# A decoder layer: the attention scores of heads 2 to 4 as three float32r products of rounded queries and keys and their remainders

## The chip, the cores and the metric

The kernel runs on one core of one Trainium2 chip. The metric is the device time of one launch in microseconds (us). The kernel before was run three times; its time is the median of these runs. One more execution was taken by the hardware profiler, and all views shown below come from it.

## The reference

One layer of a decoder over 512 tokens of 1024 features, in float32: a mixer and a feed-forward part. The mixer has two groups: four heads of an mLSTM (256 features each) and a causal depthwise convolution of 31 taps over 1024 channels. Their outputs are joined and mapped back. The part that the change touches is the mLSTM's scores:

```python
qk = silu(causal_dwconv(qk_raw, qk_conv_w, qk_conv_b))       # 4 taps
q, k = split(qk, 2)                                           # 4 heads x 256
...
scores = einsum("bhtd,bhsd->bhts", q_, k_) * exp(dmat - m_t)  # d: 256 features
num = w_inter * einsum("bhtd,bhde->bhte", q_, C) + einsum("bhts,bhse->bhte", scores, v_)
den = w_inter * einsum("bhtd,bhd->bht", q_, n) + sum(scores)
h = num / maximum(abs(den), exp(-m_t))
h = rms_norm(h, ml_norm_g) * sigmoid(o_pre)
```

The kernel computes all of this over the whole length at once (a causal matrix of 512 x 512 for each head), without the running state.

## The kernel before, in words

**Tiles and names.** A tile of the pool `slots` holds 128 partitions x 512 float32; there are 36. A head's queries are two such tiles (`q_0c`, `q_1c`: 128 features each, all 512 tokens), and its keys two (`k_2c`, `k_3c`). The code counts heads from 0, the text from 1: code head 1 is the second head. Names in profile and order carry no head's number; they repeat for each head.

**Three products for one.** Large matrix products are not done in float32. `w_split` rounds a tile to float32r (`..h`, a copy on ACT, L191) and subtracts that from the tile to get a remainder (`..l`, on POOL or DVE, L192); `mm3` then makes three float32r matmuls on PE for each pair of tiles: h x h, h x l, l x h (L210). The projections `qko` and `vo`, the glu, the output projection and the feed-forward part go this way, with the weights split as they arrive. The scores are the exception: they multiply `k` and `q` as plain float32 (L544).

**A head.** For each head PE makes the projections `qko_0` to `qko_3` (24 matmuls of 512 columns each for a stretch, 8 features' tiles x 3). `conv4` takes each from PSUM: a first step on ACT (L502, `Identity`), three steps on DVE (L504), and Silu on ACT (L505). The scores `s` are made in four blocks of keys, `s_0` to `s_3`, of 512, 384, 256 and 128 columns, each as two matmuls (one for each 128 features). DVE multiplies each with the decay matrix `E` (L545). Then come the outputs `o_0` to `o_3`, 128 tokens each, with `v` (L555). For each, ACT takes the denominator (`dm`, L558) and copies the output out of PSUM (`hn`, L559), and squares it (`junko`, L560). Later `hn` is scaled, transposed (`hT`, L586) and split into `hh` and `hl` (L592, L593).

**Banks.** The outputs `o`, the scores `s`, the transposes `hT` and the helper `Mb` take turns in two banks of PSUM (pool `at`): what is written into a bank waits for the last reader of what stood in it two turns before. So `o_2` waits for the copy `hn_0<-o_0`, and `o_3` for `hn_0<-o_1`. The projections use four other banks. The split weights take turns in 20 buffers, which are ten pieces (h and l each).

**Order.** The order of PE's instructions and of SP's (which issues most weight loads) is that of the program: the generator functions of the heads are stepped by hand, so that the outputs of one head, the gates `vo` and the projections of the next stand in turn. The orders of ACT, DVE and POOL are set when the kernel is built, by the framework's scheduler, which estimates when each operation can run. Each of these engines then works strictly in its order. DVE and POOL also do the depthwise convolution (`cv`, `cs`, `ydl`, `ysum`) in the background of the mixer, and DVE the products that make the modulation (`junk<-ada`, whose loads ACT issues).

Of the kernel before, what the change touches and what calls it, by code (L numbers as in the profile page):

```python
# [10 lines left out]
F32 = mybir.dt.float32  # L11
F32R = mybir.dt.float32r
BF16 = mybir.dt.bfloat16
AF = mybir.ActivationFunctionType
ALU = mybir.AluOpType
PSUM = bass.MemoryType.PSUM

P = 128
# [37 lines left out]
def decoder_layer(ctx, tc, w_glu0, x, c, adaT, vecs, w_glu, w_qko, w_v0, w_vo, w_out, w_up, w_down, out):  # L56
    nc = tc.nc
    V, S, G, PE = nc.vector, nc.scalar, nc.gpsimd, nc.tensor
# [31 lines left out]
    def slot(name, dt=F32):  # L90
        return slots.tile([P, T], dt, tag="t", name=name)
# [8 lines left out]
    def mmbank(name):  # L100
        return psum.tile([P, T], F32, tag="mm", bufs=4, name=name)

    def atbank(name):
        return psum.tile([P, T], F32, tag="at", bufs=2, name=name)
# [41 lines left out]
    def vcol(name, i):  # L146
        a = VEC[name][0] + i
        return vec[:, a : a + 1]
# [58 lines left out]
    def mm3(ps, a, b, start, stop, again=False):  # L207

        for i, (l, r) in enumerate(((a[0], b[0]), (a[0], b[1]), (a[1], b[0]))):
            PE.matmul(ps, l, r, start=start and i == 0, stop=stop and i == 2, skip_group_check=again)  # L210
# [97 lines left out]
    def u_tiles(name):  # L308
        hi = upool.tile([P, KT, T], F32R, tag="uh", name=f"{name}h")
        lo = upool.tile([P, KT, T], F32R, tag="ul", name=f"{name}l")  # L310
        return hi, lo, [(hi[:, j, :], lo[:, j, :]) for j in range(KT)]

    _, _, u = u_tiles("u")
# [30 lines left out]
    parts = {}  # L344
# [13 lines left out]
    for k in range(KT):  # L358
# [11 lines left out]
        hi, lo = u[k]  # L370
# [65 lines left out]
    def proj(ps, pieces, off):  # L436
        for k in range(KT):
            mm3(ps, blk(pieces, off + k), u[k], k == 0, k == KT - 1)
# [4 lines left out]
    for i in range(G0 // 2, KT):  # L443
        glu_weights(i)
        for half in range(2):
            ps = mmbank(f"glu{i}_{half}")
# [48 lines left out]
            S.activation(part_of(gate, tt), ps[:, DH:], AF.Tanh, scale=0.5)  # L495
            yield

    def conv4(ps, i, name):

        t = slot(f"{name}c")  # L500
        w = lambda tap: vcol("qk_conv_w", tap * 16 + i)
        S.activation(t, ps, AF.Identity, bias=vcol("qk_conv_b", i), scale=w(3))  # L502
        for d in range(1, 4):
            last_e[0] = V.scalar_tensor_tensor(out=t[:, d:], in0=ps[:, : T - d], scalar=w(3 - d), in1=t[:, d:], op0=ALU.mult, op1=ALU.add)  # L504
        S.activation(t, t, AF.Silu)  # L505
        return t

    hy = [None] * (2 * KT)

# [8 lines left out]
    def head_proj(h, i):  # L518

        pieces, qs, ks, so = heads[h]  # L520
        ps = mmbank(f"qko{h}_{i}")
        proj(ps, pieces, i * KT)
        e = 2 * h + i % 2
        if i < 2:
            qs.append(conv4(ps, e, f"q{h}_{i}"))
        elif i < 4:
            ks.append(conv4(ps, 8 + e, f"k{h}_{i}"))
        else:
            t = slot(f"so{h}_{i}")
            S.activation(t, ps, AF.Tanh, scale=0.5)  # L530
            so.append(t)
# [4 lines left out]
    def attention(h):  # L536

        _, qs, ks, so = heads[h]

        for cc in range(NT):  # L540
            n = NS[cc]
            sp = atbank(f"s{h}_{cc}")
            for d in range(2):
                PE.matmul(sp[:, :n], ks[d][:, cc * P : (cc + 1) * P], qs[d][:, cc * P :], start=d == 0, stop=d == 1)  # L544
            last_e[0] = V.scalar_tensor_tensor(out=E[h][cc], in0=sp[:, :n], scalar=DH**-0.5, in1=E[h][cc], op0=ALU.mult, op1=ALU.mult)  # L545
            if cc in ((0, 2, 3) if h == 0 else (1, 3)):
                yield
        ssq = small.tile([P, NT], F32, tag="ssq", name=f"ssq{h}")
        dm = small.tile([P, NT], F32, tag="dm", name=f"dm{h}")
        hn = [slot(f"hn{h}_{i}") for i in range(2)]  # L550
        for tt in range(NT):
            o = atbank(f"o{h}_{tt}")
            for cc in range(tt + 1):
                a = (tt - cc) * P
                PE.matmul(o[:, : DH + 2], E[h][cc][:, a : a + P], vs[h][cc], start=cc == 0, stop=cc == tt)  # L555
            junk = small.tile([P, DH], BF16, tag="junk2", bufs=1, name=f"junko{h}_{tt}")
            hv = hn[tt // 2][:, (tt % 2) * DH : (tt % 2 + 1) * DH]
            S.activation(dm[:, tt : tt + 1], o[:, DH : DH + 1], AF.Abs)  # L558
            S.activation(hv, o[:, :DH], AF.Copy)  # L559
            S.activation(junk, hv, AF.Square, accum_out=ssq[:, tt : tt + 1])  # L560
            if h and tt % 2:
                V.scalar_tensor_tensor(out=hn[tt // 2], in0=so[tt // 2], scalar=1.0, in1=hn[tt // 2], op0=ALU.add, op1=ALU.mult)
            if tt in (1, 2):
                yield
        rd = small.tile([P, NT], F32, tag="rd", name=f"rd{h}")
        fac = small.tile([P, NT], F32, tag="fac", name=f"fac{h}")
        V.tensor_tensor(out=dm, in0=dm, in1=em[:, :, h], op=ALU.max)
        V.reciprocal(rd, dm)
        V.scalar_tensor_tensor(out=ssq, in0=ssq, scalar=1.0 / DH, in1=rd, op0=ALU.mult, op1=ALU.mult)
        V.tensor_tensor(out=ssq, in0=ssq, in1=rd, op=ALU.mult)  # L570
        G.tensor_scalar(out=ssq, in0=ssq, scalar1=EPS, scalar2=None, op0=ALU.add)
        G.tensor_tensor(out=fac, in0=ssq, in1=mhalf, op=ALU.pow)
        if h == H - 1:
            V.tensor_tensor(out=fac, in0=fac, in1=rd, op=ALU.mult)
        for tt in range(NT):
            hv = hn[tt // 2][:, (tt % 2) * DH : (tt % 2 + 1) * DH]
            if h == H - 1:
                S.activation(hv, hv, AF.Copy, scale=fac[:, tt : tt + 1])
                continue
            V.tensor_scalar(out=hv, in0=hv, scalar1=fac[:, tt : tt + 1], scalar2=rd[:, tt : tt + 1], op0=ALU.mult, op1=ALU.mult)  # L580
        yield
        for e in range(2):
            tp = atbank(f"hT{h}_{e}")
            for tt in range(NT):
                src = hn[tt // 2][:, (tt % 2) * DH + e * P : (tt % 2) * DH + (e + 1) * P]
                PE.transpose(tp[:, tt * P : (tt + 1) * P], src, ident)  # L586
            t = tp if h else so[e]
            if not h:
                V.scalar_tensor_tensor(out=t, in0=t, scalar=1.0, in1=tp, op0=ALU.add, op1=ALU.mult)
            hi, lo = slot(f"hh{h}_{e}", F32R), slot(f"hl{h}_{e}", F32R)  # L590
            g = ghalf[:, 2 * h + e : 2 * h + e + 1]
            S.activation(hi, t, AF.Copy, scale=g)  # L592
            last_lo[0] = V.scalar_tensor_tensor(out=lo, in0=t, scalar=g, in1=hi.bitcast(F32), op0=ALU.mult, op1=ALU.subtract)  # L593
            hy[2 * h + e] = (hi, lo)
# [37 lines left out]
    def make_E(h):  # L632
# [6 lines left out]
        for cc in range(NT):  # L639
            b = ga[:, cc, h : h + 1]  # L640
            S.activation(E[h][cc][:, :P], md[:, cc * P : (cc + 1) * P], AF.Exp, bias=b, scale=-1.0)
            if cc < NT - 1:
                S.activation(E[h][cc][:, P:], mb[:, (cc + 1) * P :], AF.Exp, bias=b, scale=-1.0)
    head_load(0)
    head_proj(0, 0)
    head_proj(0, 1)

    fps = atbank("fcum")
# [4 lines left out]
    V.tensor_copy(Fc, fv)  # L653
    V.tensor_tensor(out=ga, in0=gz[:, :, :H], in1=Fc, op=ALU.subtract)
    head_proj(0, 2)

    head_proj(0, 3)
# [178 lines left out]
    for h in range(H - 1):  # L836
        head_load(h + 1)
        steps = attention(h)
        if h == 0:
            head_proj(1, 0)  # L840
# [50 lines left out]
    tc.cur_priority -= LATER  # L891
    wo = {}
    steps = attention(H - 1)
    next(steps)
    mix_first(0)
# [224 lines left out]
    for i in range(NF):  # L1120
        if i < NE:
            pa, pg = early[i]
        else:
# [12 lines left out]
            for half in range(2):  # L1136
                ps = mmbank(f"up{i}_{half}")
# [227 lines left out]
```

## Time and profile before

| | |
|---|---|
| median of 3 runs | 770.94 us (770.82 to 772.68) |
| profiled execution | 771.52 us, with a span of 769.8 us |
| PE busy | 758.5 us (99%) |
| DVE busy | 573.7 us (75%) |
| POOL busy | 522.7 us (68%) |
| ACT busy | 408.4 us (53%) |
| granted clock of PE, mean | 0.998 |
| share of the scores (L544) in the chain that ended last | 2.3% |

How to read it: busy time is summed over the whole span, so an engine with a low share can still be late at one place. A row of a timeline has the start, the length, the engine, the line of the code, the operation, what it writes and reads, and how many records it joins; in brackets stands for how long the engine was idle before it and what ended that. A float32 matmul has two records, a float32r matmul one. A row of the waits has the total, the count and the longest. A row of the table of busy time has the stretch, its length, the busy time (with counts) of PE, PE's weight loads, DVE, ACT and POOL, then the granted clock, the share of the DMA engines and GB/s.

### The profile page before, as it was taken

Reading aid. Unit: us, or ns where it says so; the run is one execution under the profiler, and the core shown is the slowest. Engines: PE = TensorE matmul, PEld = TensorE weight load, DVE = VectorE, ACT = ScalarE, POOL = GpSimd, SP = SyncE. Lnnn points to the kernel's source line nnn. Section 1 sums busy time; section 2 is a strip of 40 time slices with the busy share of each in tenths; the row PEclk is TensorE's granted clock in tenths of the full one; section 3 lists DMA queues with packets and bytes.
Section 4 is the critical chain, followed back from the end, with each engine's and each line's share of the span. In section 5 each row is a group of like instructions: output and inputs, shape, how many; then the busy total and the mean of one; then the engine's idle time right before and its main releaser. Section 6 shows DMA issues by size and latency. Waiting matters only on the chain.

```text
span 769.8 us, 10292 instructions
## 1 busy us (share of the span) xinstructions
PE 758.5 (99%) x3562; PEld 630.5 (82%) x3562; DVE 573.7 (75%) x831; ACT 408.4 (53%) x780; POOL 522.7 (68%) x432
## 2 busy tenths in 40 slices
PE   8999999999999999999999999999999999999996
PEld 6788898878788788788888998888888888888885
DVE  5669999979979696476949797675765677654548
ACT  7585438585665645573334554434445246566633
POOL 4789759795494871645611467886978786599943
PEclk9999999999999999999999999999999999999999
DMA  8973214311131250655953655856686584896273
GB/s 317 347 277 126 100 56 140 135 54 56 54 111 55 110 181 38 246 192 164 378 193 135 246 185 196 301 213 232 221 302 220 215 294 145 303 399 239 96 242 141
DMA packets 40137, 147.34 MB, mean 191 GB/s; under 512 B 3826, under 2 KB 5266, under 8 KB 30484
## 3 DMA queue, kind: packets, MB, share of 16 engines
q1 hardware_dynamic: 26372, 94.50, 34.1%
q10 hardware_dynamic: 13712, 52.18, 18.8%
q8 instruction: 28, 0.46, 0.2%
q14 instruction: 25, 0.20, 0.1%
HBM read 126.59 MB, written 20.07 MB: 191 GB/s over the span
## 4 chain that ended last, share of the span: by engine, by line
PE 91%; DMA 2%; DVE 2%; POOL 2%; issue 1%; ACT 1%; DVEq 0%; POOLq 0%; ACTq 0%
PE up L210 31%; PE qko L210 13%; PE dn L210 10%; PE vo L210 9%; PE glu L210 7%; PE mixa L210 6%; PE mixb L210 6%; PE s L544 2%; PE o L555 2%; PE glu L356 2%; PE v L210 1%; DMA p<-spill_t 1%; DMA wglu<-in_w_glu 1%; POOL wglu_0l L192 0%; PE cps L159 0%
## 5 line engine op out<-in xcount | busy, mean ns | idle before, releaser
L767 DVE SCALAR_TENSOR_TENSOR cv<-gt,cvw,cv 128x485 f32<-128x485 f32 (+23 forms) x200 | 137.1, 731 | 2.9 <-ACT cv L755 1.3
L763 POOL TENSOR_TENSOR cs<-cs,cs 128x510 f32<-128x510 f32 (+3 forms) x32 | 42.1, 1318 | 0.1
L210 PE MATMUL up<-u2l,wup_0h 128*128 128x512 f32 (+1 forms) x100 | 36.5, 365 | 0.1
L210 PE MATMUL up<-u2h,wup_0h 128*128 128x512 f32 (+1 forms) x100 | 36.5, 365 | 0.0
L210 PE MATMUL up<-u2h,wup_1024h 128*128 128x512 f32 (+1 forms) x100 | 36.4, 364 | 0.0
L210 PE MATMUL up<-u2h,wup_0l 128*128 128x512 f32 (+1 forms) x100 | 36.4, 364 | 0.0
L210 PE MATMUL up<-u2l,wup_512h 128*128 128x512 f32 (+1 forms) x100 | 36.4, 364 | 0.0
L210 PE MATMUL up<-u2h,wup_512h 128*128 128x512 f32 (+1 forms) x100 | 36.4, 364 | 0.0
L210 PE MATMUL up<-u2h,wup_1536h 128*128 128x512 f32 (+1 forms) x100 | 36.4, 364 | 0.0
L210 PE MATMUL up<-u2l,wup_1536h 128*128 128x512 f32 (+1 forms) x100 | 36.4, 364 | 0.0
L210 PE MATMUL up<-u2h,wup_1536l 128*128 128x512 f32 (+1 forms) x100 | 36.4, 364 | 0.0
L210 PE MATMUL up<-u2h,wup_512l 128*128 128x512 f32 (+1 forms) x100 | 36.4, 364 | 0.0
L210 PE MATMUL up<-u2h,wup_1024l 128*128 128x512 f32 (+1 forms) x100 | 36.4, 364 | 0.0
L210 PE MATMUL up<-u2l,wup_1024h 128*128 128x512 f32 (+1 forms) x100 | 36.3, 363 | 0.0
L176 DVE SCALAR_TENSOR_TENSOR junk<-ada,cb 128x1024 bf16<-128x1024 f32 x20 | 30.1, 1506 | 4.9 <-DMA ada<-in_adaT 4.8
L192 POOL TENSOR_TENSOR wup_0l<-wup,wup_0h 128x512 fp32r<-128x512 f32 x19 | 29.3, 1543 | 4.5 <-ACT wup_0h L191 4.5
L192 POOL TENSOR_TENSOR wup_1024l<-wup,wup_1024h 128x512 fp32r<-128x512 f32 x19 | 25.0, 1318 | 9.4 <-ACT wup_1024h L191 9.4
L192 POOL TENSOR_TENSOR wup_1536l<-wup,wup_1536h 128x512 fp32r<-128x512 f32 x19 | 27.6, 1455 | 4.7 <-ACT wup_1536h L191 4.4
L761 ACT ACTIVATE cs<-gt,cvw 128x511 f32<-128x511 f32 (+4 forms) x40 | 27.2, 712 | 6.3 <-POOL cs L763 3.8
L1099 DVE TENSOR_TENSOR b<-b 128x512 f32<-128x512 f32 x11 | 19.4, 1760 | 11.3 <-POOL b L1098 11.3
L1098 POOL TENSOR_TENSOR b<-b 128x512 f32<-128x512 f32 x11 | 14.2, 1291 | 17.3 <-DVE b L1097 17.3
L336 DVE SCALAR_TENSOR_TENSOR junk<-ada,cps 128x1024 bf16<-128x1024 f32 x16 | 19.5, 1219 | 8.3 <-ACT cb L411 4.6
(1097 smaller groups left out, 2738.5 us busy)
## 6 DMA issues: line engine op xcount, KB each, us to landing
wup<-in_w_up SPq DMA_DIRECT2D x22, 1024.0 KB, 6.0
b<-in_w_down ACTq DMA_DIRECT2D x11, 1024.0 KB, 5.1
spill_t<-b ACTq DMA_DIRECT2D x11, 1024.0 KB, 3.9
ada<-in_adaT ACTq DMA_DIRECT2D x20, 512.0 KB, 4.0
wqko<-in_w_qko SPq DMA_DIRECT2D x9, 1024.0 KB, 4.8
ada<-in_adaT SPq DMA_DIRECT2D x16, 512.0 KB, 7.2
wo<-in_w_out SPq DMA_DIRECT2D x8, 1024.0 KB, 4.8
wvo<-in_w_vo SPq DMA_DIRECT2D x6, 1024.0 KB, 4.8
```

The source lines that it names most:

```text
L176: t = V.scalar_tensor_tensor(out=junk, in0=r, scalar=1.0, in1=cb, op0=ALU.mult, op1=ALU.mult, accum_out=mod[:, i : i + 1])
L192: (eng or G).tensor_tensor(out=lo[:, :n], in0=src, in1=hi[:, :n].bitcast(F32), op=ALU.subtract)
L210: PE.matmul(ps, l, r, start=start and i == 0, stop=stop and i == 2, skip_group_check=again)
L336: V.scalar_tensor_tensor(out=junk, in0=first[k][:, i * D : (i + 1) * D], scalar=1.0, in1=cps, op0=ALU.mult, op1=ALU.mult, accum_out=part[: ...
L356: PE.matmul(ps, blk(wk, i)[a], u[k][b], start=k == 0 and p == 0, stop=k == KT - 1 and p == 1)
L544: PE.matmul(sp[:, :n], ks[d][:, cc * P : (cc + 1) * P], qs[d][:, cc * P :], start=d == 0, stop=d == 1)
L555: PE.matmul(o[:, : DH + 2], E[h][cc][:, a : a + P], vs[h][cc], start=cc == 0, stop=cc == tt)
L761: S.activation(t[:, d:], cvx[j][:, : T - d], AF.Copy, scale=w(CK - 1 - d))
L763: G.tensor_tensor(out=side[:, d:], in0=side[:, d:], in1=t[:, d:], op=ALU.add)
L767: tap = V.scalar_tensor_tensor(out=cp[:, d:], in0=cvx[j][:, : T - d], scalar=w(CK - 1 - d), in1=cp[:, d:], op0=ALU.mult, op1=ALU.add)
L1098: G.tensor_tensor(out=b12, in0=b22, in1=b12, op=ALU.subtract)
L1099: V.tensor_tensor(out=b22, in0=b22, in1=b11, op=ALU.subtract)
```

## The change

For all heads but the first, `conv4` also rounds each query and key tile on ACT (`..h`) and takes the remainder on POOL (`..l`), and the scores use `mm3`. That is four more ACT copies and four more POOL subtractions a head, and for each block of scores six float32r matmuls in the place of two float32 ones. The first head's scores stay, and what is done with scores and outputs stays.

```diff
-    def conv4(ps, i, name):
+    def conv4(ps, i, name, parts):
...
         S.activation(t, t, AF.Silu)
-        return t
+        if not parts:
+            return t
+        hi, lo = slot(f"{name}h", F32R), slot(f"{name}l", F32R)
+        S.activation(hi, t, AF.Copy)
+        G.tensor_tensor(out=lo, in0=t, in1=hi.bitcast(F32), op=ALU.subtract)
+        return hi, lo
...
-            qs.append(conv4(ps, e, f"q{h}_{i}"))
+            qs.append(conv4(ps, e, f"q{h}_{i}", h > 0))
...
-            ks.append(conv4(ps, 8 + e, f"k{h}_{i}"))
+            ks.append(conv4(ps, 8 + e, f"k{h}_{i}", h > 0))
...
-                PE.matmul(sp[:, :n], ks[d][:, cc * P : (cc + 1) * P], qs[d][:, cc * P :], start=d == 0, stop=d == 1)
+                if h:
+                    mm3(sp[:, :n], [z[:, cc * P : (cc + 1) * P] for z in ks[d]], [z[:, cc * P :] for z in qs[d]], d == 0, d == 1)
+                else:
+                    PE.matmul(sp[:, :n], ks[d][:, cc * P : (cc + 1) * P], qs[d][:, cc * P :], start=d == 0, stop=d == 1)
```

Lines after this are shifted: L544 is L552 after, L555 is L563, L558 to L560 are L566 to L568; the new copy is L509, the new subtraction L510. PE's order is otherwise the same. The scheduler gives ACT, DVE and POOL other orders. Three places of ACT's order follow, each before and after.

ACT before, at the outputs of the first head (`o_0`, `o_1`), while `conv4` works on the second head's keys `k_2` and `k_3`:

```order
L505 ACTIVATE k_2c<-k_2c 128x512
L191 ACTIVATE wqko_0_512h<-wqko_0_2143 128x512
L502 ACTIVATE k_3c<-qko_3_1860,vec 128x512
L558 ACTIVATE dm_1897<-o_0_1900 128x1
L559 ACTIVATE hn_0_1898<-o_0_1900 128x256
L558 ACTIVATE dm_1897<-o_1_1906 128x1
L559 ACTIVATE hn_0_1898<-o_1_1906 128x256
...
L505 ACTIVATE k_3c<-k_3c 128x512
L494 ACTIVATE v_1961<-vo_0_1965 128x256
```

And after:

```order
L505 ACTIVATE k_2c<-k_2c 128x512
L191 ACTIVATE wqko_0_512h<-wqko_0_2159 128x512
L509 ACTIVATE k_2h<-k_2c 128x512
L566 ACTIVATE dm_1913<-o_0_1916 128x1
L502 ACTIVATE k_3c<-qko_3_1872,vec 128x512
L566 ACTIVATE dm_1913<-o_1_1922 128x1
L505 ACTIVATE k_3c<-k_3c 128x512
L509 ACTIVATE k_3h<-k_3c 128x512
L494 ACTIVATE v_1977<-vo_0_1981 128x256
L567 ACTIVATE hn_0_1914<-o_0_1916 128x256
L567 ACTIVATE hn_0_1914<-o_1_1922 128x256
```

The two copies `hn_0` out of the banks stood before Silu of k_3c (L505), and now stand behind it, behind the new rounding k_3h, and behind the copy of `vo_0`.

ACT before, at the outputs of the second head, while the third head's `k_2` is in work:

```order
L502 ACTIVATE k_2c<-qko_2_2299,vec 128x512
L558 ACTIVATE dm_2353<-o_0_2356 128x1
L559 ACTIVATE hn_0_2354<-o_0_2356 128x256
L558 ACTIVATE dm_2353<-o_1_2362 128x1
L559 ACTIVATE hn_0_2354<-o_1_2362 128x256
...
L191 ACTIVATE wqko_0_0h<-wqko_0_2608 128x512
L505 ACTIVATE k_2c<-k_2c 128x512
```

And after:

```order
L509 ACTIVATE q_1h<-q_1c 128x512
L566 ACTIVATE dm_2397<-o_0_2400 128x1
L502 ACTIVATE k_2c<-qko_2_2339,vec 128x512
L566 ACTIVATE dm_2397<-o_1_2406 128x1
L191 ACTIVATE wqko_0_0h<-wqko_0_2656 128x512
L505 ACTIVATE k_2c<-k_2c 128x512
L191 ACTIVATE wqko_0_512h<-wqko_0_2656 128x512
L509 ACTIVATE k_2h<-k_2c 128x512
L567 ACTIVATE hn_0_2398<-o_0_2400 128x256
L567 ACTIVATE hn_0_2398<-o_1_2406 128x256
```

Here the copies `hn_0` moved behind Silu of k_2c, two pieces of the next head's weights and the rounding k_2h.

At the outputs of the third head ACT's order after the change is (before it, `hn_0<-o_0` stood right behind the first `dm`):

```order
L502 ACTIVATE k_2c<-qko_2_2824,vec 128x512
L566 ACTIVATE dm_2860<-o_0_2863 128x1
L174 DMA ada_3219<-in_adaT 128x1024
L566 ACTIVATE dm_2860<-o_1_2869 128x1
L191 ACTIVATE wo_0_0h<-wo_0_3173 128x512
L174 DMA ada_3223<-in_adaT 128x1024
L505 ACTIVATE k_2c<-k_2c 128x512
L509 ACTIVATE k_2h<-k_2c 128x512
L567 ACTIVATE hn_0_2861<-o_0_2863 128x256
```

The copy moved behind two issues of loads, a piece of the output weights (`wo`), Silu of k_2c and k_2h. At the outputs of the last head the copies keep their place, as no projections of a next head follow.

## The prediction

> **What bounds the kernel now.** I read the page first, for the share of each engine, and then the waits of PE alone.
>
> ```profile
> span 769.8 us, 10292 instructions
> PE 758.5 (99%) x3562; PEld 630.5 (82%) x3562; DVE 573.7 (75%) x831; ACT 408.4 (53%) x780; POOL 522.7 (68%) x432
> ...
> PE cps L159 <- ACT crow L158: 3.0, 1, 3.0
> PE glu L356 <- ACT uh L397: 1.1, 1, 1.1
> PE s L544 <- DVE hl L593: 0.5, 1, 0.5
> PE xT L252 <- ACT xr L304: 0.3, 1, 0.3
> ...
> 732.00:763.50 31.50, 31.50 (x140) 25.76 (x138) 20.34 (x30) 13.32 (x30) 14.62 (x12) 1.00 0.58 201
> ```
>
> PE is busy for 758.5 of 769.8 us, and the whole list of its waits is four rows with 4.9 us. After the opening one wait is left, 0.5 us. The last row above is the table of busy time for the end of the program: PE is busy for all 31.50 us of it. So this kernel is as long as PE's list of matmuls. Two things follow: a matmul that becomes shorter is won whole, and a wait of PE, anywhere, is lost whole, since no later stretch has idle PE time that could absorb it. The change does something of both kinds.
>
> **The matmuls of the scores.** The next rows are PE's timeline around the scores of head 2 (the first four: the two wide products, each with its two halves of the key; the other four: the narrow ones), and four pieces of the chain of work with start and length, for streams of equal matmuls.
>
> ```profile
> 204.76 1.02 PE L544 MATMUL s<-q_0c,k_2c 128*128 128x512 f32 x2
> 205.62 1.02 PE L544 MATMUL s<-q_1c,k_3c 128*128 128x512 f32 x2
> 206.48 0.81 PE L544 MATMUL s<-q_0c,k_2c 128*128 128x384 f32 x2
> 207.12 0.49 PE L544 MATMUL s<-q_1c,k_3c 128*128 128x384 f32 x1
> ...
> 219.56 0.59 PE L544 MATMUL s<-q_0c,k_2c 128*128 128x256 f32 x2
> 219.99 0.59 PE L544 MATMUL s<-q_1c,k_3c 128*128 128x256 f32 x2
> 220.42 0.38 PE L544 MATMUL s<-q_0c,k_2c 128*128 128x128 f32 x2
> 220.64 0.39 PE L544 MATMUL s<-q_1c,k_3c 128*128 128x128 f32 x2
> ...
> 105.92 11.52 PE v L210 x96
> 152.31 5.46 PE qko L210 x24
> 213.39 0.87 PE hT L586 x8
> ```
>
> Durations overlap in a pipeline, so I go from start to start. A float32 product of 512 columns takes 205.62 - 204.76 = 0.86 us, of 384 columns 0.64, of 256 columns 0.43, of 128 columns 0.22. Each stands twice in a head: 2 x (0.86 + 0.64 + 0.43 + 0.22) = 4.30 us.
>
> The change puts six float32r matmuls in the place of each pair. At 512 columns one takes 5.46 / 24 = 0.227 us (the projections qko). At 264 columns one takes 11.52 / 96 = 0.120 (v); I take that for 256 too. For 384 I take the middle, 0.173. At 128 columns no float32r matmul occurs here. The nearest row is hT, float32 transposes of 128 columns with a weight load each, 0.87 / 8 = 0.109; 264 columns hardly cost more than that, as if a weight load for each matmul set a floor. I take 0.107. The ends: 0.06 if the time goes on falling with the columns (half of 0.120), and 0.22 if a 128 column product costs what the float32 one does.
>
> After: 6 x (0.227 + 0.173 + 0.120 + 0.107) = 3.76 us a head. By width that is -0.36, -0.25, -0.14 and +0.20: the narrowest product gets dearer. The sum is -0.54 us a head, **-1.6 us** for heads 2 to 4; with the ends, -2.5 to +0.4.
>
> [...]
>
> **The copies and subtractions.** Twelve ACT copies (0.52 us each, from start to start, below) are 6.2 us on an engine that is idle for almost half the time, and twelve POOL subtractions (1.3 us each) 15.6 us on one with 32% idle. As sums they are covered. k_3l, the last remainder that head 2's scores need, can be made by about 190 us, and the scores start at 204.76; 14 us of cover. What is not covered is a place in ACT's queue.
>
> PE's outputs o take turns in two banks with everything else of the attention, so `o_2` needs the bank that `o_0` leaves, and that is left when ACT has copied it out (`hn_0<-o_0`). Before, that copy comes early. After the change ACT's order has the copy behind the Silu of a key tile and the new rounding `..h` of that tile, and Silu waits for a chain of three steps on DVE. This stands in the order of the built program, it is no guess; what it costs is read from three places of the trace.
>
> ```profile
> 182.28 0.62 ACT L191 ACTIVATE wqko_512h<-wqko 128x512 fp32r<-128x512 f32 x1
> 182.80 0.76 ACT L502 ACTIVATE k_3c<-qko,vec 128x512 f32<-128x512 f32 x1
> 183.46 0.15 ACT L558 ACTIVATE dm<-o 128x1 f32<-128x1 f32 x1
> 183.51 0.38 ACT L559 ACTIVATE hn<-o 128x256 f32<-128x256 f32 x1
> 187.12 0.63 ACT L505 ACTIVATE k_3c<-k_3c 128x512 f32<-128x512 f32 x1 [1.96 <-DVE k_3c L504]
> 187.66 0.37 ACT L494 ACTIVATE v<-vo 128x256 f32<-128x256 f32 x1
> 187.93 0.37 ACT L495 ACTIVATE so<-vo 128x256 f32<-128x256 f32 x1
> ...
> 183.75 0.74 DVE L504 SCALAR_TENSOR_TENSOR k_3c<-qko,vec,k_3c 128x511 f32<-128x511 f32 x1
> 186.35 0.74 DVE L504 SCALAR_TENSOR_TENSOR k_3c<-qko,vec,k_3c 128x509 f32<-128x509 f32 x1
> ...
> 185.08 1.47 PE L555 MATMUL o<-v,E 128*128 128x258 f32 x6
> ```
>
> *First head's outputs (A).* Before: hn at 183.51, done by 183.89; `o_2` starts at 185.08 and waits for nothing. After: k_2h goes in ahead of k_3c's first step, which moves from 182.80 to about 183.37 and ends 0.66 later, 184.03. DVE's chain then starts 0.28 later than at 183.75 and ends at 186.35 + 0.74 + 0.28 = 187.4 (DVE's own order around it is unchanged). Then ACT: Silu 0.54 (187.12 to 187.66), k_3h 0.52, v 0.27, hn 0.38: 189.1. `o_2` could start at 185.08. PE waits **4.0 us**. It can hardly be less than 3.5: Silu was held by DVE before too.
>
> ```profile
> 230.55 0.38 ACT L559 ACTIVATE hn<-o 128x256 f32<-128x256 f32 x1
> 235.95 0.63 ACT L505 ACTIVATE k_2c<-k_2c 128x512 f32<-128x512 f32 x1 [3.22 <-DVE k_2c L504]
> 236.49 0.61 ACT L191 ACTIVATE wqko_512h<-wqko 128x512 fp32r<-128x512 f32 x1
> ...
> 233.12 0.59 PE L555 MATMUL o<-v,E 128*128 128x258 f32 x2
> ```
>
> *Second head's outputs (B).* Before: hn done at 230.93, `o_2` at 233.12. After, the copy stands behind k_2c's Silu, wqko_512h and k_2h. The high end has Silu where it was: 235.95 + 0.54 + 0.52 + 0.52 + 0.38 = 237.9, a wait of 4.8 us. The low end: wqko_512h takes the buffers of the tenth weight piece before it, which the last matmuls of qko_3 still read, and these end as `o_2` could start; so at least 0.52 + 0.52 + 0.38 = 1.4 us. I take **1.5**: in DVE's new order two steps of the depthwise convolution (cv) and one multiplication (hn) no longer stand within or just ahead of k_2c's chain, some 3 us at 0.65 to 1.06 us each, which brings Silu to about 232.9, ahead of the buffers.
>
> ```profile
> 281.14 0.38 ACT L559 ACTIVATE hn<-o 128x256 f32<-128x256 f32 x1
> 289.13 0.63 ACT L505 ACTIVATE k_2c<-k_2c 128x512 f32<-128x512 f32 x1 [3.25 <-DVE k_2c L504]
> ...
> 284.88 1.87 DVE L176 SCALAR_TENSOR_TENSOR junk<-ada,cb 128x1024 bf16<-128x1024 f32 x1
> ...
> 286.62 0.60 PE L555 MATMUL o<-v,E 128*128 128x258 f32 x2
> ```
>
> *Third head's outputs (C).* Again k_2c's Silu and k_2h come ahead of hn. With Silu where it was: 289.13 + 0.54 + 0.52 + 0.38 - 286.62 = 3.95 us. But DVE's new order has k_2c's second step ahead of the long junk row and hn's multiplication behind the chain, 0.66 + 1.0 us less: **2.2 us** (1 to 4: the junk row waits for a DMA that ACT issues in this very queue).
>
> In the last head the copy keeps its early place, and that head's scores still wait 0.5 us for hl. The other waits that the new orders could make (`o_3`, Mb and the next scores on their banks, the scores on ..l) have some us to spare by the same reading.
>
> **The clock.** A wait of 4 us may cost more than itself. These rows are the end of the program and the opening, the same eight transposes twice:
>
> ```profile
> 764.00:766.00 2.00, 0.00 (x0) 0.00 (x0) 1.72 (x5) 0.31 (x2) 0.55 (x1) 1.00 0.70 262
> 766.00:767.00 1.00, 0.00 (x0) 0.00 (x0) 0.63 (x1) 0.00 (x0) 0.00 (x0) 0.57 0.18 68
> ...
> 8.89 1.71 PE xT L267 x8
> 11.87 0.90 PE xT L267 x8
> ```
>
> PE's last matmul starts in the stretch that ends at 763.5, and the granted clock (the third number from the end) falls to about half soon after 766, some 2.6 us later. Wait A is longer than that, B and C are not. How long the clock then stays low no row shows. In the opening PE is still at about half its speed at 8.89 us (1.71 against 0.90) and at full speed at 11.87: 3 us at half speed are seen, which cost 1.5 us. Ends: 0, if the clock does not fall, and 2.5, if a slow stretch lasts 5 us. I take **1.5**.
>
> [...]
>
> **The sum.** -1.6 + 4.0 + 1.5 + 2.2 + 1.5 = +7.6 us. The profiled execution took 771.52 us (a span of 769.8 and 1.7 around it), 0.6 above the median of the runs. Against it 779.1; against the median of 770.94, which I forecast, **778.5 us**.
>
> **The rivals.**
>
> 1. *Faster.* The scores win and PE never waits: it would need ACT to reach hn before 185.08, 233.12 and 286.62. 770.94 - 1.6 = 769.3, or 768.4 with the 0.06 us price. It decides at place A: Silu of k_3c would have to end by 183.9, but DVE's first step of that chain starts only at 183.75. 6 in 100.
> 2. *Only the first wait.* The time that PE loses at A lets DVE, which keeps working, run ahead, and B and C shrink to their lows or to nothing: 770.94 - 1.6 + 4.0 = 773.3, and 774.8 with the clock. For it speaks that DVE is 75% busy and has work lying ready; against it that the weight buffers of B do not depend on DVE. 13 in 100.
> 3. *Longer waits.* B and C keep Silu's old place: 778.5 + 3.3 + 1.8 = 783.6. The rows of DVE's order speak against it. 6 in 100.
> 4. *Dear narrow products.* If the 128 column matmul costs 0.22, the scores cost +0.4 instead of -1.6, and the time is 780.5. The hT row speaks against it. 6 in 100.
> 5. *A cheap wait.* The three waits together come to about the 1.6 us that the scores win: no difference. It would take A at a third of what I read. 5 in 100.
>
> **How the numbers follow.** The forecast has 64 in 100. The range reaches down to rival 2 without the clock, 773, and up past rival 4 and to B and C with half of their excess, 782. What a measurement of this kernel can tell from no change is 0.3%, 2.3 us. Slower by more: forecast and rivals 2, 3, 4: 0.89. Same: rival 5, 0.05. Faster by 0.3% needs rival 1 at its lower end; of its 0.06 I count 0.03 as faster and 0.03 as same.
>
> **What would show it.** In the waits of PE after: a row for `o` on ACT `hn` (line 567), three times, the longest near 4 us, about 7.7 in all. In PE's timeline: six matmuls of 512 columns in 1.36 us and of 128 columns in 0.64 us. In ACT's timeline around 187: Silu, k_3h, v, then hn. In the table of busy time a granted clock below 1 for some us after A. If no wait on hn is listed, the forecast is wrong at its root; if A is there and the clock stays full, it is 1.5 too high.

## The result, and the profile after

The changed kernel takes 790.73 us (median of four runs, 788.87 to 791.45) against 770.88 us for the kernel before on the same chip. The ratio is 1.024 (95% interval 1.022 to 1.026), slower by 19.9 us. The forecast of 778.5 us had the sign and the first mechanism; the size is far above its range. The profiled execution of the changed kernel took 788.87 us, with a span of 787.1, 17.3 us more than the span before.

First the page's busy times in the changed kernel, then its waits of PE (total, count, longest).

```profile
PE 765.0 (97%) x3586; PEld 636.7 (81%) x3586; DVE 572.8 (73%) x831; ACT 417.1 (53%) x792; POOL 535.0 (68%) x444
```

```profile
PE o L563 <- ACT hn L567: 5.9, 2, 3.2
...
PE o L563 <- DVE E L553: 2.6, 1, 2.6
PE s L210 <- DVE hl L601: 2.6, 3, 1.8
PE xT L992 <- DVE u2l L1000: 1.0, 1, 1.0
```

Left out are the opening's row `cps`, 2.9 as before, and two rows of 0.4 and 0.3. The row on `hn` is the one that was forecast, with two waits instead of three. The rows on `E`, `hl` and `u2l` were not. And PE is *busy* for 6.5 us more than before, though its products have become cheaper. That is mainly the clock. The next rows are from the table of busy time (stretch, length, then PE, weight loads, DVE, ACT, POOL, granted clock, DMA share, GB/s). The second stretch of each pair is one at half clock, and the first is the 3.41 us ahead of it:

```profile
184.36:187.77 3.41, 0.89 (x4) 0.80 (x5) 3.41 (x6) 2.74 (x8) 1.56 (x2) 1.00 0.00 0
187.77:191.19 3.42, 3.42 (x10) 2.66 (x9) 3.42 (x6) 1.47 (x7) 0.00 (x0) 0.50 0.03 7
...
228.74:232.15 3.41, 0.78 (x5) 0.32 (x3) 3.41 (x4) 0.00 (x0) 1.83 (x2) 1.00 0.00 0
232.15:235.56 3.41, 3.41 (x8) 2.76 (x9) 3.34 (x6) 0.00 (x0) 0.00 (x0) 0.50 0.00 0
...
283.35:286.76 3.41, 1.33 (x8) 0.76 (x6) 2.46 (x5) 3.38 (x7) 2.51 (x2) 1.00 0.01 2
286.76:293.59 6.83, 6.79 (x19) 5.64 (x20) 6.10 (x10) 0.52 (x2) 2.56 (x2) 0.50 0.26 77
```

Three times a stretch in which PE was busy for 0.8 to 1.3 of 3.41 us is followed by a stretch at half clock, of 3.4, 3.4 and 6.8 us. In these 13.7 us PE does about the work of 6.8: in the last of them a matmul of 512 columns starts 0.43 us after the one before it, against 0.23 at full clock.

Where PE fell behind is read from starts. In the next rows, PE in the changed kernel, each pair is the last matmul before a gap and the first after it.

```profile
183.82 0.39 PE L210 MATMUL vo<-wvo_1536h,ul 128*128 128x512 f32 x1
186.88 0.92 PE L563 MATMUL o<-v,E 128*128 128x258 f32 x3 [2.68 <-ACT hn L567]
...
229.13 0.39 PE L210 MATMUL qko<-uh,wqko_512l 128*128 128x512 f32 x1
232.15 0.80 PE L563 MATMUL o<-v,E 128*128 128x258 f32 x1 [2.63 <-DVE E L553]
...
240.45 0.39 PE L210 MATMUL qko<-uh,wqko_1536l 128*128 128x512 f32 x1
244.07 0.70 PE L563 MATMUL o<-v,E 128*128 128x258 f32 x2 [3.23 <-ACT hn L567]
...
283.33 0.39 PE L210 MATMUL qko<-uh,wqko_1536l 128*128 128x512 f32 x1
285.51 0.39 PE L210 MATMUL s<-q_0h,k_2h 128*128 128x256 f32 x1 [1.79 <-DVE hl L601]
```

A matmul of 512 columns starts 0.23 us after the one before it; what is beyond that is lost: 2.8 + 2.8 + 3.4 + 2.0 = 11.0 us. With 6.8 for the clock and 1.0 for `u2l` that is 18.8. Less about 1.3 for the cheaper products and 1.1 for the glu's wait in the opening, which is in the list of before and not in this one, 16.4 of the 17.3 us are found; the rest is small waits and rounding. The row on `u2l` isn't of the change alone: it comes with 0.6 and 0.7 us in two profiles below that lose nothing else.

The scores themselves do what they should. PE's timeline in the changed kernel, the first product of the 512 column and of the 128 column block, and the matmul that follows each block's six:

```profile
208.29 0.39 PE L210 MATMUL s<-q_0h,k_2h 128*128 128x512 f32 x1
...
209.65 0.33 PE L210 MATMUL s<-q_0h,k_2h 128*128 128x384 f32 x1
...
223.24 0.22 PE L210 MATMUL s<-q_0h,k_2h 128*128 128x128 f32 x1
...
223.86 0.45 PE L210 MATMUL qko<-uh,wqko_0h 128*128 128x512 f32 x1
```

Six of 512 columns take 209.65 - 208.29 = 1.36 us and six of 128 columns 0.62, where the prediction named 1.36 and 0.64.

**The two unforeseen waits** have one origin, the transposes `hT` of the outputs, while the next head's first query tile is in work. ACT splits `hT` into `hh`, DVE makes the remainder `hl`, and PE's next matmuls need these, or what stands behind them on DVE. ACT, DVE and POOL in the changed kernel, first head's transposes:

```profile
220.43 1.28 ACT L505 ACT_TABLE_LOAD   x1 [2.96 <-DVE q_0c L504]
221.72 0.64 ACT L505 ACTIVATE q_0c<-q_0c 128x512 f32<-128x512 f32 x1
222.39 0.63 ACT L509 ACTIVATE q_0h<-q_0c 128x512 fp32r<-128x512 f32 x1
222.93 0.71 ACT L600 ACTIVATE hh<-so,ghalf 128x512 fp32r<-128x512 f32 x1
...
223.67 7.45 DVE L601 SCALAR_TENSOR_TENSOR hl<-so,ghalf,hh 128x512 fp32r<-128x512 f32 x1 [1.13 <-ACT hh L600]
...
223.07 1.29 POOL L192 TENSOR_TENSOR wvo_1536l<-wvo,wvo_1536h 128x512 fp32r<-128x512 f32 x1
229.32 1.25 POOL L192 TENSOR_TENSOR wvo_1024l<-wvo,wvo_1024h 128x512 fp32r<-128x512 f32 x1
```

ACT has `hh` behind a table load (1.28 us), Silu and the new rounding; before, it stood right behind `q_0c`'s first step (217.01 in the trace before, with the two `hl` of 1.65 and 1.11 us right after). Then `hl` takes 7.45 us instead of 1.1 to 1.7: it ends 0.55 us after a row of POOL operations that run back to back from before its start. `E`, which the second head's `o_0` multiplies, stands behind it on DVE, and PE waits until 232.15. In the third head the late `hh` holds the scores directly (285.51).

### The profile page after: what moved, and what is told of

Same layout as the page of the kernel before. It is cut to its first block, busy times and chain, and to the rows that moved or that the text cites. A ratio compares the mean times of both kernels' runs of the same rounds, so it can differ in the third digit from the quotient of the medians.

```text
span 787.1 us, 10381 instructions
## 1 busy us (share of the span) xinstructions
PE 765.0 (97%) x3586; PEld 636.7 (81%) x3586; DVE 572.8 (73%) x831; ACT 417.1 (53%) x792; POOL 535.0 (68%) x444
## 4 chain that ended last, share of the span: by engine, by line
PE 69%; DVE 12%; DMA 7%; ACT 5%; issue 3%; POOL 3%; ACTq 0%; SPq 0%; DVEq 0%; POOLq 0%
PE up L210 31%; PE dn L210 9%; PE vo L210 8%; PE glu L210 7%; PE mixa L210 4%; DVE cv L775 4%; PE qko L210 2%; DMA wup<-in_w_up 2%; PE o L563 2%; PE glu L356 2%; DMA x<-in_x 2%; PE s L210 1%; DVE hl L601 1%; PE v L210 1%; DMA p<-spill_t 1%
## 5 line engine op out<-in xcount | busy, mean ns | idle before, releaser
L775 DVE SCALAR_TENSOR_TENSOR cv<-gt,cvw,cv 128x502 f32<-128x502 f32 (+22 forms) x200 | 136.9, 729 | 2.6 <-ACT cv L763 1.3
L563 PE MATMUL o<-v,E 128*128 128x258 f32 x80 | 21.7, 413 | 8.6 <-ACT hn L567 5.9
L563 PEld LDWEIGHTS o<-v,E 128*128 128x128 f32 x80 | 15.8, 201 | 12.8 <-ACT hn L567 7.2
```

Source lines behind the costliest of these rows:

```text
L775: tap = V.scalar_tensor_tensor(out=cp[:, d:], in0=cvx[j][:, : T - d], scalar=w(CK - 1 - d), in1=cp[:, d:], op0=ALU.mult, op1=ALU.add)
```

## The experiments

Three theories stood against each other. *Order*: the scheduler hands out the pool's tiles in the order in which the program first writes them, so new `..h` tiles that are written early push the copies `hn` and `hh` back, whether or not they bring work. *Work*: twelve more ACT copies and twelve more POOL subtractions are the cost. *Products*: the matmuls themselves are dearer.

### The products alone

The queries and keys of heads 2 to 4 are rounded in place, and their remainders are not made (each product uses the rounded tile for both), so that PE has all its new matmuls and no other engine has anything new.

```diff
-        t = slot(f"{name}c")
+        t = slot(f"{name}c", F32R if parts else F32)
...
-        hi, lo = slot(f"{name}h", F32R), slot(f"{name}l", F32R)
-        S.activation(hi, t, AF.Copy)
-        G.tensor_tensor(out=lo, in0=t, in1=hi.bitcast(F32), op=ALU.subtract)
-        return hi, lo
+        return (t, t) if parts else t
```

> The products of the change alone: heads 2 to 4 multiply rounded queries and keys three times (the remainders are left out, and the steps of the four-tap convolution write rounded values in place), so PE has the changed kernel's 36 matmuls a head at the new widths, and ACT and POOL have not one instruction more than before. If the loss comes from the orders and not from the products, the time is 769.5 us: 1.3 to 1.6 us less than before (in the changed kernel the four wide blocks took 0.55 us less and the four narrow ones 0.1 more for each head). If the products themselves cost more than their rows say, it stays above 771.

769.79 us against 771.2; the ratio is 0.998 (0.9965 to 0.9995). The waits of PE are those of the kernel before (`cps` 2.9, glu 1.0, `u2l` 0.6, `hl` 0.4). So the products bring -1.4 us (-2.7 to -0.4), and the theory that they are dearer falls.

### A new tile without new work

The remainders are left out again, and Silu writes its result, rounded, into a new tile instead of in place. No engine has an instruction more than in the kernel with the products alone.

```diff
+        if parts:
+            r = slot(f"{name}h", F32R)
+            S.activation(r, t, AF.Silu)
+            return r, r
         S.activation(t, t, AF.Silu)
-        if not parts:
-            return t
-        hi, lo = ...
+        return t
```

> As the run with the products alone, but Silu writes its rounded result into a tile of its own instead of in place (remainders left out again). No instruction is added on ACT or POOL; only one more tile is taken from the pool for each query and key. Theory order: the scheduler hands out tiles in the order in which the program first writes them, so the copies that free PE's banks stand behind Silu of the key again, and PE waits as in the changed kernel: 775 to 788 us. Rival work: the loss is the time that twelve copies and twelve subtractions take on ACT and POOL; without them nothing is lost: 769.5 us.

781.15 us (779.5 to 790.5); the ratio is 1.015 (1.009 to 1.021). Here are the waits of PE, and then the timelines of ACT at the first head's outputs (Silu is now the row that writes `k_3h`) and of DVE at its transposes:

```profile
PE o L562 <- ACT hn L566: 5.6, 3, 2.5
PE o L562 <- DVE E L552: 2.6, 1, 2.6
PE s L210 <- DVE hl L600: 1.9, 3, 1.1
```

```profile
181.16 0.22 ACT L565 ACTIVATE dm<-o 128x1 f32<-128x1 f32 x2
184.88 0.63 ACT L507 ACTIVATE k_3h<-k_3c 128x512 fp32r<-128x512 f32 x1 [3.51 <-DVE k_3c L504]
185.42 0.64 ACT L566 ACTIVATE hn<-o 128x256 f32<-128x256 f32 x2
...
220.49 7.31 DVE L600 SCALAR_TENSOR_TENSOR hl<-so,ghalf,hh 128x512 fp32r<-128x512 f32 x1 [1.24 <-ACT hh L599]
```

The same three waits are back, and the long `hl` too, with nothing added to ACT or POOL. ACT stands idle for 3.51 us ahead of Silu, with `o_0` and `o_1` ready to be copied (it has taken `dm` from both). So ACT had time for `hn`, not the turn. The work theory falls, and the order theory holds: a new tile, written early, is enough. How the scheduler comes to the new order was not looked into; that it is the handing out of tiles fits this run and the next, and is not shown beyond that. In the profiled execution the granted clock stays full to the end of the work (mean 0.998). Between the medians of this and the changed kernel lie 9.6 us, and the clock's 6.8 would be the larger part of them; the slowest of this kernel's four runs, 790.5 us, is also the one with the lowest mean clock, 0.990 against 0.994 to 0.998.

### All the work, written later

Everything of the change is kept. `conv4` only queues the two steps that split a tile; `flush` issues them after the outputs of the head before (keys) or after its transposes (first query tile).

```diff
-        S.activation(hi, t, AF.Copy)
-        G.tensor_tensor(out=lo, in0=t, in1=hi.bitcast(F32), op=ALU.subtract)
-        return hi, lo
+        def split():
+            hi, lo = slot(f"{name}h", F32R), slot(f"{name}l", F32R)
+            S.activation(hi, t, AF.Copy)
+            G.tensor_tensor(out=lo, in0=t, in1=hi.bitcast(F32), op=ALU.subtract)
+            pair.extend((hi, lo))
+        waiting.append(split)
+        return pair
...
         next(steps)
+        flush()
```

> The changed kernel with all its work (twelve copies, twelve subtractions, three products), but the program writes the rounding and the remainder of a key tile after the attention's outputs, and those of the first query tile after the transposes; ACT's order then has hn and hh about where they stood before. Theory order: the waits on hn and hl go, and the time is 769.5 to 772 us (at the third head one wait of a us or two could stay). Rival work: the same instructions cost the same time wherever they stand: 785 to 791 us.

770.18 us against 771.2; the ratio is 0.9986 (0.9977 to 0.9995). Of PE's waits one row is new, 0.5 us of `o` on `hn`; the others are those of the kernel before. Here is ACT's timeline at the first head's outputs:

```profile
184.17 0.38 ACT L582 ACTIVATE hn<-o 128x256 f32<-128x256 f32 x1
184.44 0.63 ACT L513 ACTIVATE k_2h<-k_2c 128x512 fp32r<-128x512 f32 x1
```

`hn` is back ahead of the rounding, the whole loss is gone, and the products' gain remains. This version beats both kernels, by a little. A second measurement of it, with more executions:

> The version with the splits written late once more, in more rounds beside it. Theory: as in the first time, 0.05 to 0.25% under before. Rival: the first result was chance, and the interval holds 1.

770.32 us against 771.83; the ratio is 0.9978 (0.9962 to 0.9994). The added copies and subtractions are covered, as the prediction said of their sums.

### One half at a time

If the order theory holds in detail, the keys' tiles push `hn` and the first query tile's push `hh`. In two kernels only the one or the other is written later.

```diff
+HOLD = "k"      # the other kernel: "q"
...
+        waiting.append(split)
+        if name[0] not in HOLD:
+            flush()
```

> The changed kernel with all its work, but only the key tiles' rounding is written after the attention's outputs; the query tiles' stays where the change has it, so hn comes early again and hh stays late. Theory order, piece by piece: the waits of o on hn (2.8 and 3.4 us) go; the long hl (7.4 us), PE's wait for E and the wait of the third head's scores on hl stay, each with a low clock behind it: 776 to 783 us. Rival: one of the two places carries all, 770 or 790 us.

> The other half: only the first query tile's rounding is written after the transposes (hh early), the key tiles' stays where the change has it (hn late). Theory order: hl takes 1 to 2 us, PE's wait for E and the scores' wait on hl go; the waits of o on hn stay, 2.8 us at the first head with a low clock behind it and 1.5 to 3.5 us at the second, and one at the third of up to 3: 776 to 783 us. Rival: as in the other half, 770 or 790 us.

With the keys later: 778.51 us, ratio 1.009 (1.006 to 1.012). With the queries later: 784.65 us, ratio 1.018 (1.014 to 1.021). One row of PE's waits from each, the keys' first:

```profile
PE s L211 <- DVE hl L616: 3.5, 2, 3.0
```

```profile
PE o L578 <- ACT hn L582: 9.9, 3, 4.7
```

Where the keys are written later no wait on `hn` is left, and the third head's scores wait 3.0 us for `hl`. Where the queries are, all three waits on `hn` are there (gaps of 4.9, 1.7 and 3.8 us at the places A, B and C), and `hl` is harmless. So the two kinds of waits belong to the two kinds of tiles. One thing came otherwise than expected: with the keys later the first head's long `hl` and PE's wait for `E` are gone too, though `hh` stands behind Silu and `q_0h` as in the changed kernel. DVE's row there:

```profile
221.22 1.16 DVE L616 SCALAR_TENSOR_TENSOR hl<-so,ghalf,hh 128x512 fp32r<-128x512 f32 x1 [0.88 <-ACT hh L615]
```

So a late `hh` alone doesn't make `hl` long. The losses, 6.9 and 13.1 us, add up to about that of the change, 19.9, but by chance, as their parts are not those of the changed kernel: the wait for `E` is in neither, A and C are longer than in its profile above (2.8 and 0.2 us), and B is shorter (3.4). The queries' kernel also lies a little above the 776 to 783 us that were expected. A differs from one execution to the next (below); why C and B differ no run isolates.

### The long remainder

Is the 7.45 us `hl` a matter of its operands? In the other heads the operand `hT` is in PSUM. Here the first head's gated output stays in PSUM as well; all else is as in the changed kernel.

```diff
-            t = tp if h else so[e]
+            t = tp
...
-                V.scalar_tensor_tensor(out=t, in0=t, scalar=1.0, in1=tp, op0=ALU.add, op1=ALU.mult)
+                V.scalar_tensor_tensor(out=t, in0=so[e], scalar=1.0, in1=tp, op0=ALU.add, op1=ALU.mult)
```

> The changed kernel, but the first head's gated outputs stay in the PSUM bank of their transposes instead of going back to an SBUF tile, so hl reads one operand from PSUM and one from SBUF, as it does for the other heads. Theory port: hl took 7.45 us because both operands were in SBUF while POOL ran six subtractions without a pause; now it takes 0.75, PE's wait for E (2.7 us) and the low clock behind it (1.7 us) go, and the time is 784 to 787 us. Rival: hl was long for another reason (its place, its rounding to float32r): it stays above 5 us and the time near 790.

788.06 us, ratio 1.023 (1.020 to 1.025). DVE's row at that place, then one row of the waits of PE and one of PE's timeline:

```profile
224.83 0.75 DVE L601 SCALAR_TENSOR_TENSOR hl<-hT,ghalf,hh 128x512 fp32r<-128x512 f32 x1 [1.09 <-ACT hh L600]
```

```profile
PE o L563 <- ACT hn L567: 5.6, 2, 4.8
...
225.72 0.36 PE L210 MATMUL s<-q_0h,k_2h 128*128 128x256 f32 x1 [1.83 <-DVE hl L601]
```

On the operand the answer is plain: 0.75 us, and the wait on `E` is gone. On the time the edit gave less than the expected 784 to 787 us. A has 4.8 us here, and the edit brings a wait of its own: `hl` now reads the bank of the transposes, and the second head's scores, which need that bank, wait 1.8 us for it (the last row). So this run doesn't price the long `hl` alone. What the two engines would share no run shows; the word port in the expectations is the author's guess.

A small program without the layer then put one such DVE product beside eight POOL subtractions in a row, and, in a second part, let PE idle for rising times between streams of 64 matmuls:

> Not the layer: a program of two parts that computes nothing of the reference (its output is meaningless). First part: eight times, POOL runs eight 128x512 subtractions in a row, and early in the row one DVE instruction is released. Theory port: with both operands in SBUF it waits until POOL's row is over when DVE was idle before it (about 7 to 9 us instead of 0.7), and gets its turn at the next boundary, 0.7 to 2 us, when DVE runs right up to it; with one operand in PSUM it takes 0.75. Rival: it gets its turn at the next boundary always, and the 7.45 us had another cause. Second part: streams of 64 products on PE (some 14.6 us each) with idle stretches of about 1 to 5 us between. Theory window: the granted clock falls for 3.4 us or a multiple of it, more often the longer the idle stretch, never below 1.7 us, always above 3.5 us, by chance between. Rival: a fixed length decides, the same at each repeat.

Its first part gave no long product at all: 0.98 to 1.32 us with two SBUF operands where DVE had been idle before, and 0.75 to 0.76 where DVE ran right up to it or one operand was in PSUM. A second program had longer rows on POOL, of two kinds of operation in turn:

> Not the layer: a program that computes nothing of the reference (its output is meaningless). Ten times, POOL runs a row of additions and subtractions without a pause, and after 2, 6, 10, 14, 18, 22, 26, 30, 14 and 22 of them one DVE instruction with both operands in SBUF is released, with eight more behind it on POOL. [...]

```profile
10.27 0.98 DVE L63 SCALAR_TENSOR_TENSOR hl<-so,g,hh 128x512 fp32r<-128x512 f32 x1 [4.62 <-ACT hh L62]
27.84 9.52 DVE L63 SCALAR_TENSOR_TENSOR hl<-so,g,hh 128x512 fp32r<-128x512 f32 x1 [15.79 <-ACT hh L62]
```

The rows are two of DVE's timeline in that program. Eight of ten products took 9.5 us and two 0.98. The long one shown ended at 37.36, 0.55 us after the last operation of POOL's row (36.81). What decides between the two stays open. In the changed kernel the long `hl` came when POOL had 14 operations without a pause behind it (from 205.00 on), and in the kernel before those of 1.65 and 1.11 us when it had 6 and 7; but in the small program the product after 6 operations was long and the one after 10 was not.

### The clock

The second part of the first small program answers for the clock. PE's timeline, streams of 64 equal matmuls, in brackets the idle time ahead of each:

```profile
97.85 14.80 PE L85 MATMUL bank<-w,ahi 128*128 128x512 f32 x64 [1.35 <-ACT w L91]
114.72 16.39 PE L85 MATMUL bank<-w,ahi 128*128 128x512 f32 x64 [2.07 <-ACT w L91]
217.99 17.62 PE L85 MATMUL bank<-w,ahi 128*128 128x512 f32 x64 [5.37 <-ACT w L91]
...
273.04 14.82 PE L85 MATMUL bank<-w,ahi 128*128 128x512 f32 x64 [2.73 <-ACT w L91]
```

Behind these idle times a stream took 14.80 to 14.82 us in five cases, 16.39 to 16.45 in twelve and 17.36 to 17.62 in three; the mean granted clock of the program was 0.929. By the falls in the layer the steps of 1.6 and up to 2.8 us are about one stretch of 3.41 us at half clock (1.7 us) and one of up to double length (3.4 us), an estimate. After idle times of 1.4 us none of three streams was slowed, after 2.07 us three of three, after 2.73 us one of three, from 3.39 us on all eleven. So in this program an idle time of 2 to 3 us costs itself and, in four of six cases, 1.6 us more.

What may decide there can be read in the layer. In the changed kernel the falls lie on a grid of 3.41 us (232.15 and 286.76 us are 13 and 29 times 3.41 us behind 187.77), and the outcome went with how an idle time lay on it. The wait for `E` was 2.63 us in the changed kernel, all of it in one stretch of the grid (228.74 to 232.15 above, PE busy for 0.78 us), and the clock fell. In the kernel with a new tile the same wait was 2.64 us, but an edge cuts it (first two rows, PE idle for 1.38 and 1.40 us), and the clock stayed full (1.00). B, the changed kernel's longest wait, 3.2 us, was cut in the same way (last two rows, PE idle for 1.55 and 1.68 us):

```profile
224.82:228.23 3.41, 2.03 (x9) 1.34 (x8) 3.41 (x2) 0.00 (x0) 2.43 (x2) 1.00 0.10 43
228.23:231.64 3.41, 2.01 (x8) 1.45 (x9) 3.41 (x8) 0.00 (x0) 0.00 (x0) 1.00 0.00 0
...
238.98:242.39 3.41, 1.86 (x9) 1.20 (x7) 3.41 (x6) 0.31 (x1) 1.96 (x2) 1.00 0.81 291
242.39:245.80 3.41, 1.73 (x8) 1.52 (x9) 3.41 (x7) 3.38 (x11) 2.50 (x2) 1.00 0.04 17
```

### The change once more

> The changed kernel once more, for a second profile. Theory: hl is long again (over 6 us) and PE waits at the same four places, since the orders are fixed in the program; the low clock, which depends on where a wait lies in time, may differ, so the span can be 780 to 792 us. Rival: the long hl was an accident of one execution and is not there.

A second profiled execution of the changed kernel took 792.12 us, with a span of 790.4. `hl` took 7.46 us again and the wait on `E` 2.6, but A was 4.75 us. ACT there:

```profile
187.08 0.63 ACT L505 ACTIVATE k_3c<-k_3c 128x512 f32<-128x512 f32 x1 [3.76 <-DVE k_3c L504]
...
188.54 0.65 ACT L567 ACTIVATE hn<-o 128x256 f32<-128x256 f32 x2
```

Here the clock was at half for 17.1 us, three falls of 6.8, 3.4 and 6.8 (mean granted clock 0.988, against 0.990 in the first profile). PE still waited in 1.6 us of the first, so they cost about half of 15.5, 7.7 us. The changed kernel's own executions differ in how far DVE has run ahead of PE: in the first profile Silu of `k_3c` came 2.1 us earlier, at 185.00.

### The first head as well

The version that writes the splits later, with the first head's scores as three products too:

```diff
-            qs.append(conv4(ps, e, f"q{h}_{i}", h > 0))
+            qs.append(conv4(ps, e, f"q{h}_{i}", True))
...
-                if h:
+                if True:
```

> The version with the splits written late, and the first head's scores as three products too (four more copies and subtractions). Theory: 0.43 us of PE less again and no new wait, 769.3 to 770.2 us, 0.1 to 0.25% under before. Rival: the first head's scores follow its last key tile closely, so the new rounding and remainder (0.5 and 1.25 us) make PE wait: 771 to 774 us.

780.52 us, ratio 1.010 (1.008 to 1.012): a miss. PE's waits and DVE's timeline tell why:

```profile
PE mtok L696 <- DVE Mr L689: 8.0, 1, 8.0
```

```profile
151.23 0.74 DVE L505 SCALAR_TENSOR_TENSOR k_3c<-qko,vec,k_3c 128x509 f32<-128x509 f32 x1
...
153.28 1.20 DVE L689 TENSOR_TENSOR_SCAN Mr<-aT,zero 4x512 f32<-4x512 f32 x1
```

Before, `Mr` stood ahead of `k_3c`'s steps on DVE (at 142.70); now it stands behind all three. PE waits 8.0 us, until 154.5, and from 149.84 on, still within the wait, the clock is at half for 10.2 us. It is the same kind of loss on another engine, at a place that the change had left alone. Whether writing the first head's splits still later would mend it was not tried.

## Why the prediction was right or wrong

*The scores, -1.6 us: right.* The kernel with the products alone gave -1.4.

*A, the first head's outputs, 4.0 us: right.* The order, the row in the waits and the time are as worked out: `hn` was to end at 189.1, and in the second profile it ends at 188.9 (188.54 + 0.38), for a wait of 4.75 (PE came 1 us earlier); the kernels with the queries later and with the operand in PSUM have 4.9 and 4.8. The first profile has 2.8, below the "hardly less than 3.5"; that bound failed to see that DVE can be 2 us ahead in one execution and not in another.

*B, the second head's outputs, 1.5 us: too small, 3.4.* The mechanism was right; the step that failed is "brings Silu to about 232.9", which took DVE's chain as undisturbed. DVE and ACT came to it late, with the long `hl` behind them: ACT waits 8.66 us for DVE's steps on `q_1c`, which stand behind `hl`. In the kernel with the queries later, where `hl` is harmless, B is 1.7 us.

*C, the third head's outputs, 2.2 us: 0.2 in the changed kernel.* PE had lost time just ahead of it (the wait at 285.51 and the clock behind it), and ACT reached `hn` almost in time. That is what the second rival said of B and C, and only C did it. With the query side mended C was 3.8 us, near the 3.95 of the high end.

*"The other waits that the new orders could make ... have some us to spare by the same reading": wrong, and the root of the miss.* Only `hn` was followed through ACT's new order. `hh`, the same kind of copy at the transposes, had moved too, behind a table load, Silu and the rounding. What goes with it is 2.8 us through `hl` and `E` (where the late `hh` met POOL's long row; it need not, as the kernel with the keys later shows), 2.0 us through the third head's scores, and part of B.

*The clock, 1.5 us: far too small, 6.8 and 7.7.* The first step that failed is "Wait A is longer than that, B and C are not": 2.6 us at the end of the program was read as the threshold, but it only bounds it from above. In the trace before, the granted clock stands at 1.00 through the opening, so that the slow transposes there, from which the 1.5 us were taken, are not shown to be the clock's. In the small program 2.07 us was enough three times of three, and in the layer a wait of 2.0 us at the third head's scores. That B brought no fall was right by luck: B was 3.2 us long, and was cut by an edge of the grid. The second is the number of falls: three instead of one, one of them of double length.

Together: the profiled execution lost 17.3 us where the sum had 7.6. Of the 9.7 between, the clock is 5.3, the waits behind `hh` are 4.8 and B is 1.9, while A and C gave back 1.2 and 2.0; the rest is small waits.

*The sums of copies and subtractions: right.* With the splits written later they cost nothing that these runs can tell.

Of the rivals, none came. What happened was a longer list of waits than any of them had, all from the new orders.

## What to carry to other kernels

Where one engine is busy 99% of the time, look at every copy that frees something for it, at each place where the built order has changed, and not at those alone that stand next to the new instructions; here the new tiles pushed back two kinds of copies, and much of the loss came from the one not followed. In the changed kernel a wait of PE of 2 us or more cost, besides itself, 1.7 to 3.4 us of slow clock (half of 3.41 and of 6.83) where PE was idle for 2.08 to 2.63 us of one stretch of the 3.41 us grid; where an edge cut such a wait (3.2 us into 1.55 and 1.68 there, 2.64 us into 1.38 and 1.40 in the kernel with a new tile) the clock stayed full. A forecast that doesn't know where on the grid a wait will lie can give the clock only as a chance, and as a part of its range. And where a scheduler sets the orders, write the new work in the program behind what others wait for: the same instructions, written a few steps later, turned +19.9 us into -1.0 to -1.5.

## What the runs showed of the hardware

*The clock fell after less idle time than the trace before suggested, and on a grid of 3.41 us.* In the trace before it falls behind 2.62 us of idle PE in the last 3.41 us ahead of 766.14. In the changed kernel the three falls within the work begin at 187.77, 232.15 and 286.76 us, 13 and 16 times 3.41 us apart, and last 3.42, 3.41 and 6.83 us; in the kernel with the first head as well one lasts 10.24. In the stretch of the grid ahead of these four PE was idle for 2.52, 2.63, 2.08 and 3.32 us. Of the other stretches within the work of the changed kernel, behind the opening, none was idle for more than 1.68 us, and no fall follows them. So an idle time of 2.64 us that an edge of the grid cuts passed without a fall, in the kernel with a new tile. The opening of the changed kernel does not fit: its first stretch is idle for 2.81 us, and the granted clock stays at 1.00. Nor does the kernel with the products alone: the mean granted clock of its profiled execution was 0.949, at 772.09 us and with the waits of before; where it was low was not looked into. Why a slow stretch is sometimes of double length is not settled.

*A DVE instruction with two SBUF operands took long beside some rows of POOL instructions, and ended behind the row:* 7.3 to 7.5 us in the layer and 9.5 in the small program, against 0.75 us where one operand is in PSUM. The three ends that were read against POOL's timeline (changed kernel, new tile, small program) came 0.55 us after the end of its row. It need not be: beside POOL's rows other such instructions took 1.1 to 1.9 us in the layer and 0.75 to 1.32 in the small programs. That DVE waited there for POOL is the author's reading of these times; by what means one would hold up the other was not shown.
